# Spreading a norm's factor over the partitions by a store and a broadcast load instead of matmuls with the identity, in six norms of a two-layer streaming encoder

## Chip, cores and metric

The kernel runs on one core of a Trainium2 chip. The metric is the device time of one execution in microseconds (us); lower is better. The engines are TensorE (PE), VectorE (DVE), ScalarE (ACT), GpSimd (POOL) and SyncE (SP), which here issues the DMAs. The line numbers in the text are those of the kernel before, L163 for line 163, unless it says otherwise.

## What is computed

Two layers of an encoder over 1056 tokens (1024 of a prompt and 32 of a sample) of width 1024, in float32. Around each layer's mixer stand two norms: one of the layer's input, and one of its output before the residual is added. These norms are what the change touches.

```python
def rmsnorm(x, g):
    xf = x.astype(jnp.float32)
    y = xf * lax.rsqrt(jnp.mean(xf * xf, axis=-1, keepdims=True) + RMS_EPS)
    return (y * g.astype(jnp.float32)).astype(x.dtype)
...
    for layer in range(DEPTH):
        if layer % 2 == 0:
...
            yp, pp, kp, vp = even_mixer(rmsnorm(xp, norm_pre[layer]), *wts)
...
        else:
...
            yp, cp, np_, mp = odd_mixer(rmsnorm(xp, norm_pre[layer]), *wts)
...
        xp = xp + rmsnorm(yp, norm_post[layer])
```

The even layer's mixer is a combined input projection, a pooling branch and a chunk-band attention, then an output projection; the odd layer's is an input projection, an mLSTM and an output projection.

## The kernel before

Activations lie transposed: the 1024 channels as eight blocks of 128 partitions, the tokens along the free dimension. The tokens are worked on in three groups, GR: two of 384 tokens (group 0 and 1) and one of 288 (group 2). A float32 matrix product is made of three matmuls, L108 to L110: activations and weights are split into a high and a low part (xh, xl and wh, wl), and xh by wh, xl by wh and xh by wl are summed in PSUM.

A norm needs, for each token, r = 1 / sqrt(mean of squares + eps), and needs it on every partition, since tokens lie along the free dimension and r multiplies the 128 channels of a block.

- The squares of the eight blocks are added up as they come: ACT squares (L193, tiles sqt and th), POOL adds to the tile acc (L194). This is `sumsq`.
- `rnorm_p` then sums over the partitions on PE: with acc as the stationary operand and one column of ones, each 128 tokens give one column of 128 sums (L163). The tokens now lie on the partitions. DVE makes mean + eps (L170, L172, tile rn_a), and `rsqrt` takes POOL's power of -0.5 (L182, rn_b) and one Newton step on DVE (L183 to L185). At the end of L185 the tile y, or rn_b, holds r, token 128 c + p on partition p in column c.
- To bring r back on the free dimension and onto all partitions, PE multiplies once for each 128 tokens: column c of y, broadcast to 128 columns, is the stationary operand and the identity the moving one (L176). Every partition of the PSUM tile pm then holds r of the tokens. `rnorm` copies it to SBUF on ACT (L153), into the tile rp or r.

Two kinds of norm call this outside the first layer's input. `out_proj` makes one for each group behind the output projection: at k = 0 of the group's second pass it calls `rnorm` into rp (L804), and each of the eight blocks y is then multiplied by rp (L808), the residual x0, loaded at L807, is added (L809), and `finish` is called. This second pass runs while PE already works on the next group. In layer 0, `finish` is `fin0` (L1166): it stores the new x to DRAM (L1172, x1d), splits it for the next layer's projection (L206 xh, L209 xl), adds up its squares, and after the eighth block calls `rnorm` for the next layer's input norm, into the tile r1 (L1176, r in the trace). r1 is not applied to x but to the projection's result in PSUM, when DVE evacuates it (L263, L265). In layer 1, `finish` is `fin1`: it stores the result (L1180, out_y). Group 2 of layer 1 takes another way, `out_last` (L813), with x0 loaded at L820.

At the boundary of the layers, three more things matter. `gate_rows` (L837) multiplies the new x of each group with the weights of the gates, sixteen matmuls a group (L846, L847), and the PSUM tile is evacuated by a copy on ACT (L849) and an addition on DVE (L850). The weights come in blocks of 128 x 512 by a load on SP (L94, wr), a conversion on ACT (L95, wh) and a subtraction on DVE or POOL (L96, wl); the gates' own weights are split at L835 and L836. And each engine works its instructions off in the order in which the scheduler put them; it places an instruction by what it expects to be ready, so an edit to one norm can shift the order of its neighbours. SP's queue is in order too: a store that waits for its data holds back every load behind it.

Of the kernel before, what the change touches and what calls it, by code (L numbers as in the profile page):

```python
# [7 lines left out]
F32 = mybir.dt.float32  # L8
# [25 lines left out]
class Net:  # L34
    def __init__(self, tc, io):
        self.tc = tc
        self.nc = tc.nc
        self.io = io
        self.due = []
        self.store = None  # L40


# [106 lines left out]
        return xh, xl  # L149


    def rnorm(self, acc, n, out, col=None, pool=None):
        self.nc.scalar.copy(out=out, in_=self.rnorm_p([acc], n, col, pool))  # L153

    def rnorm_p(self, accs, n, col=None, pool=None):
        nc = self.nc
        p = self.pn.tile([128, 512], F32, name="pm") if pool is None else pool.tile([128, 512], F32, name="pv")
        nf, rem = n // 128, n % 128
        nq = nf + (rem > 0)
        for c in range(nq):  # L160
            L = min(128, n - 128 * c)
            for i, acc in enumerate(accs):
                nc.tensor.matmul(out=p[:L, 400 + c:401 + c], lhsT=acc[:, 128 * c:128 * c + L], rhs=self.ones[:, 0:1],  # L163
                                 start=i == 0, stop=i == len(accs) - 1)
        ms = self.tp.tile([128, 4], F32, name="rn_a", bufs=2)
        y = self.tp.tile([128, 4], F32, name="rn_b", bufs=2) if col is None else col
        u = self.tp.tile([128, 4], F32, name="rn_c", bufs=2)
        if rem:
            nc.vector.memset(ms, 1.0)
            nc.vector.tensor_scalar(out=ms[:rem, nf:nq], in0=p[:rem, 400 + nf:400 + nq], scalar1=1.0 / 1024, scalar2=1e-6,  # L170
                                    op0=ALU.mult, op1=ALU.add)
        nc.vector.tensor_scalar(out=ms[:, :nf], in0=p[:, 400:400 + nf], scalar1=1.0 / 1024, scalar2=1e-6, op0=ALU.mult, op1=ALU.add)  # L172
        self.rsqrt(y[:, :nq], ms[:, :nq], u[:, :nq])
        for c in range(nq):
            L = min(128, n - 128 * c)
            nc.tensor.matmul(out=p[:, 128 * c:128 * c + L], lhsT=y[:L, c:c + 1].to_broadcast([L, 128]), rhs=self.ident[:L, :L],  # L176
                             start=True, stop=True)
        return p[:, :n]
# [554 lines left out]
    def out_proj(self, wsrc, gpost, late, resid, finish, ytiles=(), nx0=4, nopen=2, end=False, w2=2, anchor=None):  # L733
        nc = self.nc
        tc = self.tc
        mv = self.mix.rearrange("(k p) t -> p k t", p=128)
        early = [k for k in range(8) if k not in late]
        steps = []
        ws = []
        ytiles = list(ytiles)  # L740
        for gi in range(3):
            s, n = GR[gi]
            x = self.new_x(gi)
            for k in early + list(late):
                if k in late:
                    src = late[k][:, s:s + n]
                else:
                    xr = self.tp.tile([128, 384], F32, name="xr", bufs=4)
                    with tc.issue_after(wdma) if gi and 1 else nullcontext():
                        nc.sync.dma_start(out=xr[:, :n], in_=mv[:, k, s:s + n])  # L750
                    src = xr[:, :n]
                with tc.issue_after(anchor) if gi and anchor is not None else nullcontext():
                    self.split_x(x, k, src, None, nc.gpsimd if gi < 2 and k % 2 == 0 else None)
            acc = self.tp.tile([128, 384], F32, name="acc", bufs=2)
            ys = []
            accs = [acc[:, :n]]

            def evac(m, p):
                if gi == 0 and ytiles:
                    y = ytiles.pop(0)  # L760
                else:
                    y = self.lp.tile([128, 384], F32, name="y", bufs=11)
                ys.append(y)
                if end and gi == 2 and m == 7:
                    sq = self.tp.tile([128, 384], F32, name="sqt", bufs=2)
                    nc.scalar.activation(out=sq[:, :n], in_=p, func=AF.Square)
                    accs.append(sq[:, :n])
                else:
                    self.sumsq(acc[:, :n], p, n, m == 0)
                nc.scalar.mul(out=y[:, :n], in_=p, mul=gpost[:, m:m + 1])  # L770
            batches = [list(range(nopen))] + [[m] for m in range(nopen, 8)] if gi == 0 else [[m] for m in range(8)]
            for ms in batches:
                opened = []
                for m in ms:
                    while gi == 0 and len(ws) <= min(ms[-1] + 1, 7):
                        i = len(ws)
                        ws.append(self.load_w(wsrc[i], None if i < 2 else w2 if i == 2 else i))
                        if i == 6:
                            wdma = self.wdma
                        if i == 4 and self.store is not None:  # L780

                            with tc.issue_after(self.wdma):
                                self.store()
                            self.store = None
                    w = ws[m]
                    p = (self.pn.tile([128, 512], F32, name="pm") if gi == 0 and m == 3 and end else self.pd.tile([128, 512], F32, name="pd"))[:, :n]
                    self.mm3(p, w, x, early, True, False)
                    opened.append((m, w, p))
                for m, w, p in opened:
                    self.mm3(p, w, x, list(late), False, True)  # L790
                    evac(m, p)
                for _ in range(2):
                    if steps:
                        steps.pop(0)()
            while steps:
                steps.pop(0)()
            if end and gi == 2:
                self.out_last(ys, accs, resid, s, n, finish)
                return
            r = self.lp.tile([128, 384], F32, name="rp", bufs=1)  # L800

            def one(k, gi=gi, s=s, n=n, ys=ys, acc=acc, r=r):
                if k == 0:
                    self.rnorm(acc[:, :n], n, r[:, :n])  # L804
                y = ys[k][:, :n]
                x0 = self.lp.tile([128, 384], F32, name="x0", bufs=nx0)
                nc.sync.dma_start(out=x0[:, :n], in_=resid[128 * k:128 * k + 128, s:s + n])  # L807
                nc.vector.tensor_tensor(out=y, in0=y, in1=r[:, :n], op=ALU.mult)  # L808
                nc.vector.tensor_tensor(out=y, in0=y, in1=x0[:, :n], op=ALU.add)  # L809
                finish(gi, k, y)  # L810
            steps = [lambda k=k, one=one: one(k) for k in range(8)]
        return steps

# [340 lines left out]
    def run(self):  # L1154
        tc, nc, io = self.tc, self.nc, self.io
        with tc.tile_pool(name="cp", bufs=1) as self.cp, tc.tile_pool(name="xp", bufs=1) as self.xp, \
# [8 lines left out]
            accs = {}  # L1165

            def fin0(gi, k, y):
                s, n = GR[gi]
                if k == 0:
                    x1[gi] = self.new_x(gi)  # L1170
                    accs[gi] = self.tp.tile([128, 384], F32, name="acc", bufs=2)
                nc.sync.dma_start(out=x1d[128 * k:128 * k + 128, s:s + n], in_=y)  # L1172
                self.split_x(x1[gi], k, y, self.g_pre[1])
                self.sumsq(accs[gi][:, :n], y, n, k == 0, None, "th")
                if k == 7:
                    self.rnorm(accs[gi][:, :n], n, r1[:, s:s + n])  # L1176

            def fin1(gi, k, y):
                s, n = GR[gi]
# [2 lines left out]
            with tc.tile_pool(name="la", bufs=1, reuse_waits="tile") as self.la:  # L1182
                with tc.tile_pool(name="lq", bufs=1, reuse_waits="tile") as self.lq:
# [4 lines left out]
                    with tc.tile_pool(name="lp0b", bufs=1, reuse_waits="tile") as self.lp, tc.tile_pool(name="pn", bufs=2, reuse_waits="tile", space=PSUM) as self.pn:  # L1188
                        next(l0)
                        r1 = self.tp.tile([128, T], F32, name="r", bufs=1)  # L1190
# [100 lines left out]
```

## Time and profile before

| what | value |
| --- | --- |
| median of three runs | 1215.55 us (1214.6 to 1216.65) |
| the profiled execution, its own time | 1215.28 us |
| its span, first to last instruction | 1213.6 us |
| mean granted clock of PE, as a share of full speed | 0.991 |
| PE busy | 1183.3 us, 98% |
| DVE, ACT, POOL busy | 681.2, 472.9, 298.9 us |

Busy times of engines overlap. An engine that is idle costs nothing unless the chain that ended last runs through it. PE's matmuls are pipelined: one of 384 columns is listed with 0.33 us, but the next begins 0.17 us after it.

### The profile page before, as it was taken

To read this page: it belongs to the slowest core of one execution; us is meant where nothing else is said; L and a number is where in the kernel's file an instruction comes from. 1 tells how busy PE (TensorE), PEld (TensorE's weight loads), DVE (VectorE), ACT (ScalarE), POOL (GpSimd) and SP (SyncE) were. 2 spreads that over 40 slices of the span, in tenths; PEclk is the share of its full clock that TensorE was granted. 3 is DMA by queue.
4 is the path that set the end of the run, shared out by engine and by line. 5 is a ranking of instruction groups with operands and counts; after the bars stand their busy time and mean duration, and the time that the engine had idled before them with its cause. 6 is when DMAs were issued, how large, how long until landed. Compare 5 with 4: busy or idle time off the path is not lost.

```text
span 1213.6 us, 19521 instructions
## 1 busy us (share of the span) xinstructions
PE 1183.3 (98%) x7457; PEld 1137.1 (94%) x7457; DVE 681.2 (56%) x1460; ACT 472.9 (39%) x980; POOL 298.9 (25%) x394
## 2 busy tenths in 40 slices
PE   7899999999999899999999999999999999999996
PEld 7899899898899799999999899999999999998996
DVE  7657476576668446774447533753247432666424
ACT  7624334443533454531334232432234322445521
POOL 1323532433241335620102300221003110123322
PEclk9999999999999999999999899999999999999998
DMA  8401121112212253321111231122111321122433
GB/s 257 125 19 54 54 82 53 54 45 67 78 36 92 80 176 105 124 94 53 54 36 53 63 101 36 52 67 98 36 51 42 76 88 36 44 77 79 128 104 130
DMA packets 79613, 94.03 MB, mean 77 GB/s; under 512 B 19208, under 2 KB 56856, under 8 KB 79520
## 3 DMA queue, kind: packets, MB, share of 16 engines
q1 hardware_dynamic: 79520, 92.79, 24.9%
q8 instruction: 58, 0.95, 0.3%
q14 instruction: 35, 0.29, 0.1%
HBM read 72.64 MB, written 21.69 MB: 78 GB/s over the span
## 4 chain that ended last, share of the span: by engine, by line
PE 95%; ACT 1%; DMA 1%; DVE 1%; issue 1%; POOL 1%; SPq 0%; DVEq 0%; POOLq 0%; ACTq 0%
PE pd L108 25%; PE pd L110 25%; PE pd L109 25%; PE pv L406 4%; PE ps L354 1%; PE pm L950 1%; PE ps L355 1%; PE ps L1018 1%; PE pv L985 1%; PE pv L987 1%; PE pv L986 1%; PE ps L985 1%; PE ps L986 1%; PE ps L987 1%; PE pm L176 1%
## 5 line engine op out<-in xcount | busy, mean ns | idle before, releaser
L108 PE MATMUL pd<-xh,wh 128*128 128x384 f32 (+1 forms) x1864 | 610.2, 328 | 9.4 <-ACT wh L95 7.8
L110 PE MATMUL pd<-xh,wl 128*128 128x384 f32 (+1 forms) x1864 | 607.5, 326 | 0.1
L109 PE MATMUL pd<-xl,wh 128*128 128x384 f32 (+1 forms) x1864 | 607.1, 326 | 0.1
L108 PEld LDWEIGHTS pd<-xh,wh 128*128 128x128 f32 x1864 | 352.4, 189 | 13.6 <-ACT wh L95 8.1
L109 PEld LDWEIGHTS pd<-xl,wh 128*128 128x128 f32 x1864 | 352.6, 189 | 2.6 <-POOL xl L203 0.3
L110 PEld LDWEIGHTS pd<-xh,wl 128*128 128x128 f32 x1864 | 352.3, 189 | 2.4 <-DVE wl L96 0.7
L95 ACT CAST wh<-wr 128x512 fp32r<-128x512 f32 x158 | 91.4, 619 | 154.6 <-PE pd L109 109.6
L96 DVE TENSOR_TENSOR wl<-wr,wh 128x512 fp32r<-128x512 f32 x116 | 78.2, 701 | 22.1 <-ACT wh L95 20.5
L96 POOL TENSOR_TENSOR wl<-wr,wh 128x512 fp32r<-128x512 f32 x42 | 55.7, 1342 | 83.4 <-DMA extr<-ext 27.4
L194 POOL TENSOR_TENSOR acc<-acc,sqt 128x384 f32<-128x384 f32 (+1 forms) x41 | 43.5, 1062 | 88.2 <-ACT sqt L193 88.1
L1032 POOL TENSOR_TENSOR qal<-qa,qah 128x256 fp32r<-128x256 f32 (+1 forms) x32 | 27.5, 863 | 141.1 <-ACT qah L1031 130.3
L75 POOL TENSOR_SCALAR_AFFINE_SELECT D<-D 128x128 f32<-128x128 f32 (+1 forms) x36 | 12.2, 340 | 181.2 <-ACT D L1014 168.1
L406 PE MATMUL pv<-st,vt 128*128 128x512 f32 (+1 forms) x192 | 55.1, 433 | 0.9 <-ACT rg L415 0.9
L406 PEld LDWEIGHTS pv<-st,vt 128*128 128x128 f32 x192 | 35.0, 189 | 20.3 <-issue 10.6
L263 DVE TENSOR_TENSOR row<-pd,r 128x384 f32<-128x384 f32 (+1 forms) x36 | 18.3, 520 | 59.4 <-PE pd L110 59.3
L372 ACT ACTIVATE st<-ps,far 128x256 f32<-128x256 f32 (+3 forms) x56 | 27.1, 489 | 50.0 <-DVE st L364 34.0
L1050 DVE SCALAR_TENSOR_TENSOR C<-C,MA,ps 128x258 f32<-128x258 f32 x64 | 30.4, 478 | 28.8 <-PE ps L987 17.8
L265 DVE SCALAR_TENSOR_TENSOR kT<-pd,r 128x384 f32<-128x384 f32 (+1 forms) x24 | 12.6, 524 | 57.4 <-PE pd L110 57.3
L395 DVE TENSOR_TENSOR st<-st,mb 128x512 f32<-128x512 f32 (+1 forms) x96 | 39.3, 485 | 8.3 <-POOL mb L699 8.3
L1030 POOL TENSOR_TENSOR qa<-qT,MA 128x128 f32<-128x128 f32 (+1 forms) x64 | 26.9, 439 | 66.1 <-DVE qT L263 35.9
L364 DVE TENSOR_TENSOR st<-ps,B 128x256 f32<-128x256 f32 (+1 forms) x72 | 25.3, 371 | 24.7 <-PE ps L355 24.3
L1085 ACT ACTIVATE hn<-num,n_u,n_y 128x256 f32<-128x256 f32 (+1 forms) x36 | 20.4, 596 | 40.9 <-PE pv L1087 34.3
(305 smaller groups left out, 1681.5 us busy)
## 6 DMA issues: line engine op xcount, KB each, us to landing
wr<-in_w SPq DMA_DIRECT2D x128, 256.0 KB, 3.0
xr<-mix SPq DMA_DIRECT2D x26, 192.0 KB, 2.5
wr<-in_w0o SPq DMA_DIRECT2D x16, 256.0 KB, 3.2
MA<-mdr SPq DMA_DIRECT2D x32, 128.0 KB, 3.5
wr<-in_w1o SPq DMA_DIRECT2D x16, 256.0 KB, 3.3
x<-in_x SPq DMA_DIRECT2D x16, 192.0 KB, 2.8
x<-x1d SPq DMA_DIRECT2D x16, 192.0 KB, 3.5
out_y<-y SPq DMA_DIRECT2D x16, 192.0 KB, 2.0
```

The costliest lines, as they stand in the source:

```text
L95: nc.scalar.copy(out=wh[:, k], in_=wr)
L96: eng.tensor_tensor(out=wl[:, k], in0=wr, in1=wh[:, k].bitcast(F32), op=ALU.subtract)
L108: nc.tensor.matmul(out=p, lhsT=wh[:, k], rhs=xh[:, k], start=first and i == 0, stop=False)
L109: nc.tensor.matmul(out=p, lhsT=wh[:, k], rhs=xl[:, k], start=False, stop=False)
L110: nc.tensor.matmul(out=p, lhsT=wl[:, k], rhs=xh[:, k], start=False, stop=last and i == len(ks) - 1)
L194: (eng or nc.gpsimd).tensor_tensor(out=acc, in0=acc, in1=t[:, :n], op=ALU.add)
L372: nc.scalar.activation(out=st[:, off + a:off + b], in_=p[:, a:b], func=AF.Identity, bias=far)
L395: nc.vector.tensor_tensor(out=dst, in0=dst, in1=mb[:, a - q0:b - q0], op=ALU.subtract)
L406: nc.tensor.matmul(out=pv[:, a - q0:b - q0], lhsT=vt[:, j, 64 * e:64 * e + 128], rhs=dst, start=(i == 0), stop=(i == len(order) - 1))
L1030: nc.gpsimd.tensor_tensor(out=qa[:, d, :L], in0=qT[:, d, t], in1=Ab, op=ALU.mult)
L1032: nc.gpsimd.tensor_tensor(out=qp[1], in0=qa[:, :, :L], in1=qp[0].bitcast(F32), op=ALU.subtract)
L1050: nc.vector.scalar_tensor_tensor(out=Cn[:, d], in0=C[:, d], scalar=Ab[:, L - 1:L], in1=pu, op0=ALU.mult, op1=ALU.add)
```

## The change

In two places, for groups 0 and 1 alone, `rnorm` is replaced by `rnorm_far`. It runs `rnorm_p` up to the end of the Newton step (a new argument, `spread=False`, returns there), into a tile of its own, rn_d. Then it stores the 128 x 3 numbers to a row of 384 numbers in DRAM, in the order of the tokens, so that each number goes to a place of its own, and loads this row into rp or r1 on all 128 partitions, a broadcast of 192 KB. Both DMAs are issued by SP. The matmuls of L176 and the copy of L153 are gone for these norms: six of them, groups 0 and 1 of the output norm of layer 0, of the input norm of layer 1 and of the output norm of layer 1. Group 2 and the first layer's input norms stay as they are.

```diff
@@ -37,6 +37,7 @@
         self.due = []
+        self.nfar = 0
         self.store = None
@@ -149,10 +150,23 @@
+    def rnorm_far(self, acc, n, out):
+        nc = self.nc
+        y = self.tp.tile([128, 4], F32, name="rn_d", bufs=2)
+        self.rnorm_p([acc], n, y, spread=False)
+        nf, rem = n // 128, n % 128
+        row = self.dr.tile([1, 384], F32, name=f"rfar{self.nfar}")
+        self.nfar += 1
+        nc.sync.dma_start(out=row[0, 0:128 * nf].rearrange("(c p) -> p c", p=128), in_=y[:, :nf])
+        if rem:
+            nc.sync.dma_start(out=row[0, 128 * nf:n].rearrange("(p c) -> p c", c=1), in_=y[:rem, nf:nf + 1])
+        nc.sync.dma_start(out=out, in_=row[0:1, 0:n].to_broadcast([128, n]))
+
     def rnorm(self, acc, n, out, col=None, pool=None):
         self.nc.scalar.copy(out=out, in_=self.rnorm_p([acc], n, col, pool))
 
-    def rnorm_p(self, accs, n, col=None, pool=None):
+    def rnorm_p(self, accs, n, col=None, pool=None, spread=True):
@@ -171,6 +185,8 @@
         self.rsqrt(y[:, :nq], ms[:, :nq], u[:, :nq])
+        if not spread:
+            return
         for c in range(nq):
@@ -801,7 +817,7 @@
                 if k == 0:
-                    self.rnorm(acc[:, :n], n, r[:, :n])
+                    (self.rnorm_far if gi < 2 else self.rnorm)(acc[:, :n], n, r[:, :n])
@@ -1173,7 +1189,7 @@
                 if k == 7:
-                    self.rnorm(accs[gi][:, :n], n, r1[:, s:s + n])
+                    (self.rnorm_far if gi < 2 else self.rnorm)(accs[gi][:, :n], n, r1[:, s:s + n])
```

The changed kernel's lines are 1 to 16 further down (its L161 is the store, its L164 the load). What moves on the engines' queues beyond that is shown at three places.

SP's queue between the two norms that stand 7 us apart, the layer-1 input norm of group 0 and the layer-0 output norm of group 1. Before:

```order
L1172 DMA x1d<-y 128x384
L807 DMA x_4829<-in_x 128x384
L94 DMA wr<-in_w 128x512 x3
L1172 DMA x1d<-y 128x384 x4
L807 DMA x_4869<-in_x 128x384
```

After:

```order
L823 DMA x_4826<-in_x 128x384
L161 DMA rfar_4565<-rn_d 128x3x1
L164 DMA r<-rfar_4565 128x384
L95 DMA wr<-in_w 128x512 x2
L161 DMA rfar_4762<-rn_d 128x3x1
L95 DMA wr<-in_w 128x512
L164 DMA rp<-rfar_4762 128x384
L1188 DMA x1d<-y 128x384 x4
```

Both pairs stand ahead of the next stores of x; a weight load stands between the second store and its load.

PE's queue at the sums over the partitions of the layer-1 input norm of group 0 (pm<-ones,acc). Before:

```order
L108 MATMUL pd<-xh_4306,wh_4236 128x384
L109 MATMUL pd<-xl_4307,wh_4236 128x384
L110 MATMUL pd<-xh_4306,wl_4237 128x384
L108 MATMUL pd<-xh_4306,wh_4236 128x384
L109 MATMUL pd<-xl_4307,wh_4236 128x384
L163 MATMUL pm<-ones,acc 128x1 x3
L110 MATMUL pd<-xh_4306,wl_4237 128x384
```

After:

```order
L110 MATMUL pd<-xl_4307,wh_4197 128x384
L111 MATMUL pd<-xh_4306,wl_4198 128x384
L109 MATMUL pd<-xh_4306,wh_4236 128x384
L110 MATMUL pd<-xl_4307,wh_4236 128x384
L111 MATMUL pd<-xh_4306,wl_4237 128x384
L109 MATMUL pd<-xh_4306,wh_4236 128x384
L110 MATMUL pd<-xl_4307,wh_4236 128x384
L177 MATMUL pm<-ones,acc 128x1 x3
L111 MATMUL pd<-xh_4306,wl_4237 128x384
```

The sums now stand behind five matmuls of the weight block 4236 instead of fourteen, so nine matmuls earlier. On POOL, the additions of squares are reordered alike: one addition of sqt (L194) that stood ahead of the norm's last addition now stands behind it. The sums of the next norm, of group 1, stand six matmuls of 288 columns further back than before, and those of the layer-1 input norm of group 1 four matmuls of 384 columns further back.

PE's queue at the gate rows of groups 0 and 1 (x of group 0 is xl_4388 and xh_4387 before). Before:

```order
L163 MATMUL pm<-ones,acc 32x1
L108 MATMUL pd<-xh_5119,wh 128x288
L109 MATMUL pd<-xl_5120,wh 128x288
L110 MATMUL pd<-xh_5119,wl 128x288
L847 MATMUL pd<-xh_4387,wh 128x384
L846 MATMUL pd<-xl_4388,wh 128x384
L847 MATMUL pd<-xh_4387,wh 128x384
L846 MATMUL pd<-xl_4388,wh 128x384
L847 MATMUL pd<-xh_4387,wh 128x384
L846 MATMUL pd<-xl_4773,wh 128x384
```

After, where group 1's x is xl_4770 and xh_4769:

```order
L110 MATMUL pd<-xl_5116,wh 128x288
L111 MATMUL pd<-xh_5115,wl 128x288
L862 MATMUL pd<-xl_4770,wh 128x384
L863 MATMUL pd<-xh_4769,wh 128x384
L862 MATMUL pd<-xl_4770,wh 128x384
L863 MATMUL pd<-xh_4769,wh 128x384
```

Before, the last five matmuls of group 0's gate rows stood directly ahead of group 1's. Now all sixteen of group 0 stand in one piece further ahead, and group 1's follow a stretch of group 2's projection. On ACT, the evacuation of group 1's gate rows (L849) now stands behind a fourth conversion of weights (L95), where it stood ahead of it.

## Rows read from the trace of the kernel before

**Rows 1.** The page: busy time of PE; the chain that ended last, by engine.

```profile
PE 1183.3 (98%) x7457; PEld 1137.1 (94%) x7457; DVE 681.2 (56%) x1460; ACT 472.9 (39%) x980; POOL 298.9 (25%) x394
...
PE 95%; ACT 1%; DMA 1%; DVE 1%; issue 1%; POOL 1%; SPq 0%; DVEq 0%; POOLq 0%; ACTq 0%
```

**Rows 2.** Instructions of L176: count of records, duration ns min/median/max, first and last start.

```profile
L176 PE MATMUL pm<-ident,rn_b x54: 271/275/376, 456.5 to 1205.0; 128*128 128x128 f32 x48, 32*128 32x32 f32 x6
```

**Rows 3.** The chain in order of time, 440 to 560 us: start us, us, what.

```profile
456.68 0.67 PE pm L176 x6
...
478.75 0.83 PE pm L163 x6
...
513.04 1.51 PE pm L163 x12
```

**Rows 4.** Timeline of DVE: start us, us, line, operation, [idle before <-releaser].

```profile
457.90 2.43 DVE L808 TENSOR_TENSOR qT<-qT,rp 128x384 f32<-128x384 f32 x5 [4.76 <-ACT rp L153]
...
488.36 0.16 DVE L185 SCALAR_TENSOR_TENSOR rn_b<-rn_c,rn_b 128x3 f32<-128x3 f32 x1
...
492.34 3.99 DVE L808 TENSOR_TENSOR y<-y,rp 128x384 f32<-128x384 f32 x7 [1.95 <-ACT rp L153]
...
513.07 0.56 DVE L263 TENSOR_TENSOR qT<-pd,r 128x384 f32<-128x384 f32 x1 [1.73 <-PE pd L110]
...
515.43 0.16 DVE L185 SCALAR_TENSOR_TENSOR rn_b<-rn_c,rn_b 128x3 f32<-128x3 f32 x1
...
520.66 0.56 DVE L263 TENSOR_TENSOR qT<-pd,r 128x384 f32<-128x384 f32 x1 [4.23 <-ACT r L153]
...
1184.76 2.58 DVE L808 TENSOR_TENSOR y<-y,rp 128x384 f32<-128x384 f32 x4 [4.09 <-ACT rp L153]
```

**Rows 5.** Timeline of SP's issues and of ACT at a store and its broadcast load.

```profile
587.69 0.32 SPq L931 DMA_DIRECT2D mdr<-num  x1
...
589.94 1.41 SPq L1010 DMA_DIRECT2D MA<-mdr  x3
...
593.25 0.40 ACT L1014 ACTIVATE D<-MA,g_c 128x128 f32<-128x128 f32 x1 [5.56 <-DMA MA<-mdr]
```

**Rows 6.** DMA issues of the whole span: count, KB each, median us to landing.

```profile
xr<-mix SPq DMA_DIRECT2D x26, 192.0 KB, 2.5
...
extr<-ext SPq DMA_DIRECT2D x8, 192.0 KB, 4.1
...
out_uo<-u SPq DMA_DIRECT2D x8, 7.5 KB, 2.6
...
mix<-smo SPq DMA_DIRECT2D x4, 16.0 KB, 1.4
```

**Rows 7.** Timelines of POOL and PE around the sums of the layer-1 input norms.

```profile
476.07 1.34 POOL L194 TENSOR_TENSOR acc<-acc,sqt 128x384 f32<-128x384 f32 x1
477.37 1.33 POOL L194 TENSOR_TENSOR acc<-acc,th 128x384 f32<-128x384 f32 x1
...
511.98 1.01 POOL L194 TENSOR_TENSOR acc<-acc,th 128x384 f32<-128x384 f32 x1
...
478.33 0.34 PE L109 MATMUL pd<-xl,wh 128*128 128x384 f32 x1
```

**Rows 8.** Timeline of DVE: the split of the gates' weights.

```profile
489.70 0.69 DVE L836 TENSOR_TENSOR wh<-wr,wh 128x512 fp32r<-128x512 f32 x1 [1.18 <-ACT wh L835]
```

**Rows 9.** Timelines of PE, ACT and DVE at the gate rows.

```profile
539.93 0.44 PE L846 MATMUL pd<-xl,wh 128*128 128x384 f32 x1 [1.15 <-DVE row L850]
...
540.49 0.62 ACT L95 CAST wh<-wr 128x512 fp32r<-128x512 f32 x1 [1.19 <-DMA wr<-in_w]
...
543.55 0.55 DVE L850 TENSOR_TENSOR row<-pd,row 64x384 f32<-64x384 f32 x1 [1.71 <-ACT row L849]
```

**Rows 10.** Timeline of ACT in group 2 of the last projection.

```profile
1192.30 1.04 ACT L770 ACTIVATE y<-pd,vec 128x288 f32<-128x288 f32 x2 [0.57 <-DMA out_y<-y]
1194.48 0.41 ACT L193 ACTIVATE sqt<-pd 128x288 f32<-128x288 f32 x1 [1.15 <-PE pd L110]
```

## The prediction

> **What bounds the kernel now.** I read the page's busy table and chain first [rows 1]: TensorE (PE) is busy 98% of the span and makes 95% of the chain that ends last. An instruction taken off PE's queue therefore shortens the kernel by its own time, unless a wait takes its place. Next, what the change removes. The matmuls with the identity, line 176, that use this kind of norm have 54 records, six for each of nine norms [rows 2]; on the chain, one norm's six cost 0.67 us (456.68) [rows 3]. Six norms change; I call them A, C, B, D (at 453, 481, 488 and 515 us: group 0 of layer 0's post-norm, group 0 of layer 1's pre-norm, then the same two for group 1) and E, F (layer 1's post-norm, 1146 and 1180 us). If nothing else moved, the gain would be 6 x 0.67 = 4.0 us.
>
> Then I looked at who waits for r. VectorE (DVE) does nothing between the norm's last step, L185, and the first use of r [rows 4]: from 453.14 to 457.90 us for A (4.76), 488.52 to 492.34 for B (3.82), 515.59 to 520.66 for D (5.1) and 1180.66 to 1184.76 for F (4.1). C's r is first used at 513.07, some 30 us after its norm. E is of A's kind. In these waits the norm stands behind other matmuls in PE's queue; PE's own share is 0.67, and ACT copies the result. So the question is what a store and a load take, against 3.8 to 5.1 us.
>
> **The price of the round trip.** No row of this trace shows a 1.5 KB store spread over 128 partitions in 4-byte pieces, so X, the time from L185's end to a usable r, is bounded. The nearest row is the same idiom: a 16.5 KB store at 587.69, the broadcast load that reads it issued at 589.94 (2.25 later), and ScalarE (ACT) released by it at 593.25 (3.31 after that) [rows 5]: 5.56 us. That load was one of several in flight; here it is alone. A load of the same 192 KB without broadcast takes 2.5 us (xr) [rows 6], which makes 2.25 + 2.5 = 4.75. I take **X = 5.2**, the middle of these two. The far bounds: the fastest small store, 1.4, and xr make 3.9; the store that is made of the smallest pieces, out_uo with 2.6, and the 192 KB broadcast extr with 4.1 make 6.7 [rows 6].
>
> **The change, step by step.** I keep a ledger: PE's time after the change minus before, at the same work.
>
> A: its matmuls go, -0.67. Its r comes 5.2 - 4.76 = 0.44 later, and the chain y*r, plus residual, square, add follows.
>
> C: its sums, line 163, wait for GpSimd's (POOL) last add, which ended at 477.37 + 1.33 = 478.70, with PE there at about 478.5, its last matmul having begun at 478.33 [rows 7]. In the new order these sums stand nine matmuls of 0.172 us earlier (1.55) and one square's add (1.34) fewer stands ahead of the last one. PE arrives at 478.5 - 0.67 - 1.55 = 476.3; the add ends at 478.70 - 1.34 + 0.44 = 477.8. PE waits 1.5 us, and with the nine matmuls still to do it stands at 477.8 + 1.55 - 478.75 = **+0.6**. A's gain is gone here. C's own matmuls then go: -0.1.
>
> B: its sums now stand behind six more matmuls of 288 columns, at three quarters of 0.172 each, 0.8 in all. y is ready at 488.52 + 0.7, r at 494.4, which is 2.1 later than before. On SyncE's (SP) queue a weight load that waits for L836's split at 489.70 [rows 8] now stands between store and load; it ends at 490.4, before the store has landed (489.2 + 2.25), so I cost it at nothing. If the store landed sooner than that, it would hold the load. Weight loads may share the transfer's time with it; the upper bound of X holds that. B's matmuls go: -0.75.
>
> D: its sums had no slack at all: POOL's last add ended at 511.98 + 1.01 = 512.99 and PE went on at 513.04 [rows 3, 7]. Of B's 2.1 us about 0.4 is taken up by POOL's queue, where the last adds of the squares stand back to back; the sums start at 514.7, and four matmuls (0.69) that came behind them are now ahead: 514.7 - 513.04 - 0.69 = **+1.0**. D's own matmuls go: +0.3. D's r comes at 515.59 + 1.66 + 5.2 = 522.45, 1.8 later, and DVE, which idles for it (4.23), starts group 2's residual work that much later.
>
> The gate rows: PE stood idle 1.15 us at 539.93 for an evacuation of the gate rows [rows 9]. The new order puts all sixteen matmuls of group 0's gate rows ahead of other work, and that stall should go: -0.85. But the next pair is held by ACT: line 849 of group 1 now stands behind a fourth weight conversion, which at 540.49 waits for its load. And what follows group 2's gate rows, the first k matmuls, now waits for those rows' evacuation, a copy and an add of about 0.45 each for 288 columns. Before, they waited for no evacuation, and the one at 543.55 (0.55 for 384 columns) stood ahead of the sixteen [rows 9]. So a wait of about 0.9 behind takes the place of one in front; it comes out even if the sixteen start at 543.2 instead of 544.1, and by the shifts above I have them start between 543.2 and 543.7. I put A to D together at **+0.1** (-0.2 to +0.5).
>
> E: r 0.4 later, but what waits for it is a multiplication and the stores of y, beside group 1's projection, whose matmuls fill the 30 us up to F: **-0.67**. F: r comes 5.2 - 4.1 = 1.1 later. The stores of y follow it, and ACT's evacuation in group 2 already waits for one of them at 1192.30 (0.57) [rows 10]; the first of those two evacuations ends at 1192.82, and PE takes that buffer again at 1194.48, where the tile before ended: 1.66 to spare, 1.0 when PE is 0.67 ahead. So 0.1 is lost: **-0.6**. The ACT copies (one for each norm), and twelve DMA issues on SP, which issues nothing in most of the time here, cost nothing as long as nothing behind a waiting store is due; behind F's stand loads of group 2's residual, not needed for 15 us.
>
> Sum: 0.1 - 0.67 - 0.6 = -1.2 us. The profiled run took 1215.28 us (span 1213.6), 0.3 under the median of the runs: **1214.1**. A measurement of this kernel tells 0.2%, 2.4 us, from no change: the forecast is no change.
>
> **Rivals.** Each us of X is worth about 3 us above 5.2: A's delay reaches C's sums and through PE also B's norm, B's reaches D's sums, and F's reaches PE; below 5.2 it is about 2, since F's and part of B's are then hidden.
>
> (1) The round trip is short and hidden. At X = 4.0, about the low bound, A and F wait no longer than before, and the time is 1214.1 - 2 x 1.2 = 1211.7. Everything hidden and the stalls at C and 539.93 gone too would be 4.0 + 0.25 + 1.15 = 5.4, or 1209.9. For it: DVE waited 3.8 to 5.1 us already. Against: the one round trip in the trace took 5.56. The Trainium skill, "DMA: Bandwidth & Descriptors", section "Anatomy of one DMA — SWDGE (gpsimd) path", gives a fixed cost of about 2.0 us for each transfer, and by it two small ones would take about 4.0; the rows here lie above that, 2.25 and 2.5 to 4.1. Chance 0.28.
>
> (2) Slower: the store in 4-byte pieces is dear. The store's 384 pieces are three times out_uo's (128 partitions with 60 bytes each; its 7.5 KB takes 2.6 us where 192 KB of xr take 2.5 [rows 6], so pieces and not bytes set it). With 3.2 for the store and the broadcast's 3.5 to 4.1, X is 6.7 to 7.3. At 6.7, 1.5 x 3 = 4.5 comes on top: 1218.6. It is slower from X = 6.4 on (-1.2 + 3 x 1.2 = 2.4). Its place is B's r and D's sums at 513. The Trainium skill, same page, section "Rules for kernel authors", speaks against this change: a transfer whose last dimension is strided becomes one descriptor per element. No row here shows the price of that. Chance 0.22.
>
> (3) The order of PE, not X, decides: the sums moved nine matmuls earlier cost the 1.5 us stall, and the 1.15 at 539.93 doesn't go, or comes back behind the gate rows. Then A to D come to +1.2 and the time is 1215.2: no change either. Chance 0.12.
>
> That the matmuls stay can be excluded: PE's order has 18 of them fewer, in six places.
>
> **How the numbers follow.** My forecast has 0.38. No change within 0.2%: 0.38 + 0.12 less the tails, 0.48; faster 0.30, since the forecast's lower tail adds 0.02; slower 0.22. The range takes X from 4.0 with some of the stalls gone (1211.7 - 1.0) to 6.5 (1214.1 + 3.9): 1210.7 to 1218.0.
>
> **What would show it.** Line 176's 54 records should fall to 18. DVE's idle before L808 (A, B) and L263 (D) should read 5.2, and B's use of r start at about 494. PE should wait about 1.5 us before C's sums, near 476 to 478, and as long before D's. The stall at the gate rows of 539.93 should be gone and a smaller one stand ahead of the first k matmuls. Outside 440 to 560 us and the last 70 us both traces should agree. X under 4.5 or over 6.4 makes the forecast wrong, and so does a stall of PE of over 2 us anywhere behind D.

## The result, and the profile after

The changed kernel takes 1260.62 us (median of 4 runs, 1259.16 to 1261.74) beside 1216.05 us before: a ratio of 1.0364 (95% interval 1.0348 to 1.0379), 45 us slower, where no change was forecast. Its profiled execution has a span of 1258.6 us and a mean granted clock of 0.974.

The page of the changed kernel, busy times and chain; beside [rows 1] PE's share of the chain falls from 95% to 78%, and DMA has 11%:

```profile
PE 1192.7 (95%) x7421; PEld 1143.2 (91%) x7421; DVE 675.0 (54%) x1460; ACT 469.0 (37%) x974; POOL 296.8 (24%) x394
...
PE 78%; DMA 11%; DVE 5%; ACT 3%; issue 2%; POOL 1%; SPq 1%; DVEq 0%; ACTq 0%; POOLq 0%
```

The matmuls went as said: 36 records fewer. What took their place is in the view of DMA issues (count, KB each, median us from issue to landing):

```profile
rp<-rfar SPq DMA_DIRECT2D x4, 192.0 KB, 4.9
...
rfar<-rn_d SPq DMA_DIRECT2D x6, 1.5 KB, 8.4
```

The store of 1.5 KB lands after 8.4 us, the load takes 4.9: X, the time from the norm's end to a usable r, is 13.3, where 5.2 was taken and 6.7 was the far bound. DVE's idle time before the first use of r is about that long, 12.5 to 15.9 us, on the lines that answer to [rows 4] (norms A, B, D and F; idle in brackets). B's is the longest; its store took 11.8 us.

```profile
467.57 2.43 DVE L824 TENSOR_TENSOR qT<-qT,rp 128x384 f32<-128x384 f32 x5 [13.58 <-DMA rp<-rfar]
...
516.10 3.84 DVE L824 TENSOR_TENSOR y<-y,rp 128x384 f32<-128x384 f32 x8 [15.92 <-DMA rp<-rfar]
...
553.17 0.56 DVE L279 TENSOR_TENSOR qT<-pd,r 128x384 f32<-128x384 f32 x1 [12.49 <-DMA r<-rfar]
...
1229.60 2.90 DVE L824 TENSOR_TENSOR y<-y,rp 128x384 f32<-128x384 f32 x6 [13.74 <-DMA rp<-rfar]
```

PE stands idle six times where it did not before (timeline of PE, idle in brackets):

```profile
476.18 0.44 PE L109 MATMUL pd<-xh,wh 128*128 128x384 f32 x1 [3.89 <-ACT y L786]
486.03 0.83 PE L177 MATMUL pm<-ones,acc 128*128 128x1 f32 x6 [2.96 <-POOL acc L210]
...
524.54 0.61 PE L109 MATMUL pd<-xh,wh 128*128 128x288 f32 x1 [12.81 <-ACT y L786]
...
557.67 1.24 PE L109 MATMUL pd<-xh,wh 128*128 128x288 f32 x2 [5.95 <-ACT xh L222]
...
1200.47 0.44 PE L109 MATMUL pd<-xh,wh 128*128 128x384 f32 x1 [1.73 <-ACT y L786]
...
1236.45 0.61 PE L109 MATMUL pd<-xh,wh 128*128 128x288 f32 x1 [7.44 <-ACT y L786]
```

Four of the six wait for ACT's evacuation L786, that is for a free PSUM buffer. The two of them at the boundary of the layers, 476.18 and 524.54, have one cause: ACT takes its instructions in order, and there the next one was the split of the late x (timeline of ACT for the longer stall; the evacuation is the second line). The two in layer 1, 1200.47 and 1236.45, have another, the buffers y, which the experiments show. Of the other two, the stall at 486.03 stands at C's sums, and the one at 557.67 waits for group 2's x, which DVE makes behind its wait for D's late r.

```profile
520.44 0.61 ACT L222 ACTIVATE xh<-y,vec 128x384 fp32r<-128x384 f32 x1 [14.60 <-DVE y L825]
...
524.00 0.87 ACT L786 ACTIVATE y<-pd,vec 128x288 f32<-128x288 f32 x2
```

And behind each stall PE runs slower. The view of windows (PE busy and records, granted clock, DMA share, GB/s) shows clocks between 0.60 and 0.84 around the stalls, where 1.0 is the upper of the two levels, 2.4 GHz, and 0.5 the lower, 1.2 GHz; the matmul of 288 columns at 524.54 is listed with 0.61 us, where those of the kernel before take 0.30 in the mean:

```profile
470.00:480.00 10.00, 6.11 (x28) 0.84 0.55 178
480.00:490.00 10.00, 7.04 (x34) 0.84 0.44 138
510.00:520.00 10.00, 1.72 (x13) 0.72 0.24 21
520.00:530.00 10.00, 5.46 (x29) 0.60 0.61 207
```

**Where the 45 us are.** PE's idle time (span less busy) rises from 30.3 to 65.9 us, by 35.6. Its busy time rises by 9.4, though 4.0 us of matmuls are gone, so the matmuls that are left take 13.4 longer: 35.6 + 13.4 - 4.0 = 45.0. The six stalls above make 34.8 of the 35.6. By place: the sums over the partitions are landmarks on the chain in order of time. In the kernel before, those of B and E:

```profile
485.69 0.56 PE pm L163 x6
...
1144.38 0.56 PE pm L163 x6
```

and after, B, D (the one that answers to 513.04 in [rows 3]) and E:

```profile
496.26 0.56 PE pm L177 x6
...
537.58 0.58 PE pm L177 x6
...
1177.89 0.58 PE pm L177 x6
```

The lag is 10.6 us at B's sums (A's late r), 24.5 at D's (B's added), 33.5 at E's (D's added) and 45.0 at the end (E's and F's). Some 0.75 of it stood at A's sums already, before any r was late (451.39 against 450.64).

### The profile page after: what moved, and what is told of

Its sections match the earlier page's. It is cut to its first block, busy times and chain, and to the rows that moved or that the text cites. A ratio compares the mean times of both kernels' runs of the same rounds, so it can differ in the third digit from the quotient of the medians.

```text
span 1258.6 us, 19464 instructions
## 1 busy us (share of the span) xinstructions
PE 1192.7 (95%) x7421; PEld 1143.2 (91%) x7421; DVE 675.0 (54%) x1460; ACT 469.0 (37%) x974; POOL 296.8 (24%) x394
## 4 chain that ended last, share of the span: by engine, by line
PE 78%; DMA 11%; DVE 5%; ACT 3%; issue 2%; POOL 1%; SPq 1%; DVEq 0%; ACTq 0%; POOLq 0%
PE pd L109 21%; PE pd L110 20%; PE pd L111 20%; PE pv L422 4%; DMA rfar<-rn_d 4%; DMA rp<-rfar 2%; DMA MA<-mdr 1%; DMA wr<-in_w 1%; PE ps L370 1%; PE pm L966 1%; PE ps L371 1%; PE ps L1034 1%; PE pv L1001 1%; PE pv L1003 1%; PE pv L1002 1%
## 5 line engine op out<-in xcount | busy, mean ns | idle before, releaser
L76 POOL TENSOR_SCALAR_AFFINE_SELECT D<-D 128x128 f32<-128x128 f32 (+1 forms) x36 | 12.5, 348 | 180.8 <-ACT D L1030 168.4
L1066 DVE SCALAR_TENSOR_TENSOR C<-C,MA,ps 128x258 f32<-128x258 f32 x64 | 30.3, 477 | 29.7 <-PE ps L1003 17.3
L380 DVE TENSOR_TENSOR st<-ps,B 128x256 f32<-128x256 f32 (+1 forms) x72 | 25.4, 371 | 25.8 <-PE ps L371 25.3
L824 DVE TENSOR_TENSOR y<-y,rp 128x384 f32<-128x384 f32 (+1 forms) x33 | 15.1, 527 | 43.0 <-DMA rp<-rfar 43.0
```

The source lines that it names most:

```text
L1066: nc.vector.scalar_tensor_tensor(out=Cn[:, d], in0=C[:, d], scalar=Ab[:, L - 1:L], in1=pu, op0=ALU.mult, op1=ALU.add)
```

## The experiments

Twelve kernels were run; each group had runs of the kernel before beside it. Four causes were to be told apart: the store's small pieces, any round trip through DRAM, SP's queue, and the new order on PE.

**What makes the store late.** One unused store behind each norm, in six shapes (A to F and the others in turn):

```diff
+        if i % 6 == 0:
+            out, src = row[0:384].rearrange("(c p) -> p c", p=128), y[:, 0:3]
+        elif i % 6 == 1:
+            out, src = row[0:384].rearrange("(p c) -> p c", c=3), y[:, 0:3]
+        elif i % 6 == 2:
+            out, src = row[0:128].rearrange("(p c) -> p c", c=1), y[:, 0:1]
+        elif i % 6 == 3:
+            out, src = row.rearrange("(c p s) -> p c s", p=128, s=16)[:, :, 0], y[:, 0:3]
...
+        self.nc.sync.dma_start(out=out, in_=src)
```

> The kernel before, with one extra store behind each of its nine norms that nobody reads or waits for, in six shapes: 384 pieces of 4 bytes side by side (as in the change), 128 pieces of 12 bytes side by side, 128 pieces of 4 bytes, 384 pieces of 4 bytes each 64 bytes from the next, 3 pieces of 512 bytes, 128 pieces of 12 bytes each 64 bytes apart. Theory (the small pieces make the store slow to land): the first shape lands in 8.4 us here too, the 128 pieces in 2.5 to 4, the 3 pieces in about 2; if the 384 spread pieces also take 8, their number decides, if they take 2 to 3, that neighbours share a place in DRAM. The time stays within 2.4 us of before, since nobody waits. Rival (any small store of r lands this late, because of what else runs on the DMA engines then): all shapes 7 to 9 us.

The trace shows a landing for four of the stores (DMA issues in short windows, in order of time):

```profile
prb<-rn_b SPq DMA_DIRECT2D x1, 1.5 KB, 3.0
...
prb<-rn_b SPq DMA_DIRECT2D x1, 0.5 KB, 6.9
...
prb<-rn_b SPq DMA_DIRECT2D x1, 1.5 KB, 3.2
...
prb<-rn_b SPq DMA_DIRECT2D x1, 1.5 KB, 2.1
```

The first and the last are 128 pieces of 12 bytes side by side (3.0 and 2.1), the second 128 pieces of 4 bytes side by side (6.9, where 2.5 to 4 was expected), the third 384 pieces of 4 bytes, each 64 bytes from the next (3.2). The change's own shape and the last two of the list show no landing in this run. With a load behind it that nobody uses (the unused pair, below), the change's own shape lands after 7.8 to 8.2 us in five of six places. So it is not the number of pieces that makes the store late, since 384 spread ones land in 3.2 (one store, with no other DMA beside it), but that 4-byte pieces are neighbours. The 6.9 fits this but decides nothing: the DMA engines were 81% busy with weight loads then. The time was 1218.9 us, ratio 1.003 (1.0019 to 1.0041), a little more than expected; where these 2.5 us went was not followed.

**The same change with a faster store.** The sums take every third token, so that a partition holds three neighbours:

```diff
-        self.rnorm_p([acc], n, y, spread=False)
+        self.rnorm_p([acc[:, :n].rearrange("q (p c) -> q c p", c=3)], n, y, spread=False)
...
-        nc.sync.dma_start(out=row[0, 0:128 * nf].rearrange("(c p) -> p c", p=128), in_=y[:, :nf])
+        nc.sync.dma_start(out=row[0, 0:128 * nf].rearrange("(p c) -> p c", c=3), in_=y[:, :nf])
```

> The changed kernel with the sums over the partitions taken of every third token, so that a partition holds three neighbouring tokens and the store is 128 pieces of 12 bytes instead of 384 of 4. Nothing else is different. Theory (pieces): the store lands in 3 to 4 us instead of 8.4, r comes 8 to 9 us after its norm instead of 13.3, and of the 45 us lost some 10 to 15 are left: 1225 to 1232. Rival (a store and a dependent load through DRAM cost this much in any shape, or the new order of PE is what costs): 1255 to 1262.

1225.51 us, ratio 1.0074 (1.0048 to 1.0100). DMA issues:

```profile
rp<-rfar SPq DMA_DIRECT2D x4, 192.0 KB, 4.0
...
rfar<-rn_d SPq DMA_DIRECT2D x6, 1.5 KB, 2.2
```

With 6 us taken off the store, 35 of the 45 us are gone, with the sums of the changed norms on PE within one matmul of the change's order: the pieces make most of the loss, not the order and not the round trip as such. But 9 us are left at X = 6.2 to 6.5. The windows say in what:

```profile
470.00:480.00 10.00, 7.46 (x44) 1.00 0.59 190
480.00:490.00 10.00, 10.00 (x57) 0.83 0.16 22
```

PE idles 6.3 us more than before (36.6 against 30.3), and its matmuls take 8.9 us longer, behind stalls of no more than 2.6 us. Not all of this is the clock: the sums of every third token take PE 0.32 us more a norm (shown below for E's), some 1.9 us for six. How much of the 9 us is the new order on PE was not separated from the rest.

**SP's queue alone.** The kernel before with the store and load at the six places, into a tile that nobody reads:

```diff
+        if col is None and n == 384:
+            self.pair(y)
...
+    def pair(self, y):
+        row = self.dr.tile([1, 384], F32, name=f"rfar{self.nfar}")
...
+        nc.sync.dma_start(out=row[0, 0:384].rearrange("(c p) -> p c", p=128), in_=y[:, :3])
+        nc.sync.dma_start(out=d, in_=row[0:1, 0:384].to_broadcast([128, 384]))
```

> The kernel before, r still made by the matmuls with the identity, and at the six changed norms the same store and broadcast load on SP's queue besides, into a tile that nobody reads. Theory (r's lateness costs, and SP's queue only little): within 5 us of before, 1214 to 1220, since what stands behind the pair on SP's queue is late by up to 9 us but mostly has that much to spare. Rival (SP's queue: stores of x, residual loads and weight loads held behind the waiting load are what stops PE): 1235 or more, over half of the 45 us.

1227.81 us, ratio 1.0096 (1.0074 to 1.0119): over twice what the theory allowed, and still a quarter of the 45 us. It lies between what the theory and the rival said. One stall makes most of it. Timelines of SP, ACT and PE:

```profile
491.19 0.39 SPq L188 DMA_DIRECT2D rfar<-rn_b  x1
502.67 0.33 SPq L189 DMA_DIRECT2D rdead<-rfar  x1
503.09 0.38 SPq L95 DMA_DIRECT2D wr<-in_w  x1
503.56 1.90 SPq L1183 DMA_DIRECT2D x1d<-y  x4
...
509.06 0.50 ACT L781 ACTIVATE y<-pd,vec 128x288 f32<-128x288 f32 x1 [7.90 <-DMA x1d<-y]
...
509.61 0.61 PE L109 MATMUL pd<-xh,wh 128*128 128x288 f32 x1 [6.79 <-ACT y L781]
```

r was in time here. But the load waits for the store on SP, the stores of x stand behind the load, and ACT's evacuation needs a buffer y that such a store must first empty. This is a second way in which the slow store can reach PE, and it was costed at nothing. In the changed kernel it is hidden: ACT there waits for the late x itself (520.44 above), so these 11.4 us are not to be added to what the late r costs. B's store took 11.5 us between its issue and the load's (11.8 in the changed kernel), where A's took 7.8; two weight loads had been issued directly before it.

**Layer 1's two norms alone, and what stops PE there.**

```diff
-                    (self.rnorm_far if gi < 2 else self.rnorm)(acc[:, :n], n, r[:, :n])
+                    (self.rnorm_far if gi < 2 and end else self.rnorm)(acc[:, :n], n, r[:, :n])
```

with the layer-1 input norms back at `rnorm`.

> The change in the two output norms of layer 1 alone; the four norms at the boundary of the layers keep the matmuls. Theory (each late r stops PE by itself, as the trace after shows: up to the sums of the first of these two norms the changed kernel is 33.5 us behind, at its end 45): 45 - 33.5 = 11.5 us over before, 1225 to 1229. Rival (the new order of PE and ACT at the boundary costs the rest of the kernel, too): 1214 to 1218.

1227.6 us, ratio 1.0095 (1.0074 to 1.0116), 11.2 over before, as expected. To this kernel, matmuls without use were added where PE idled:

```diff
+                    if end and gi == 2 and m == 6:
+                        idle = self.pn.tile([128, 512], F32, name="pm")
+                        self.mm3(idle[:, :n], w, x, range(8), True, True)
+                        self.mm3(idle[:, :n], w, x, range(5), True, True)
                     self.mm3(p, w, x, early, True, False)
```

> The kernel with the change in layer 1's two output norms alone, and 39 extra matmuls of 288 columns ahead of the seventh product of group 2, where PE then stood idle for 6.4 us; their result is not used. Theory (a stall of PE costs twice, by itself and by the lower clock behind it): the extra matmuls take 5.4 us of the stall at 0.137 us each and lengthen nothing; the granted clock from 1200 to 1210 us, 0.62 to 0.70 without them, stays near 1.0, and the two products behind the stall take 6.6 us instead of 8.7, so 1224.5 to 1226 against 1227.6 without them. Rival (the stall alone costs; the clock falls with what DMA and the other engines do there): the clock falls as before and the time is 1227.6 or more.

1225.27 us, ratio 1.0073 (1.0056 to 1.0091); the spans are 1225.5 without and 1222.4 with the 39 extra matmuls, but 0.9 of these 3.1 us stood ahead of this stage already. The stall falls from 6.40 to 1.55 us, and from its end to the sums of the last norm it is 7.2 us instead of 9.2 (1202.97 to 1210.19, and 1203.56 to 1212.75). Windows without them:

```profile
1200.00:1205.00 5.00, 1.44 (x6) 0.62 0.64 228
1205.00:1210.00 5.00, 5.00 (x29) 0.70 0.93 286
```

and with them:

```profile
1200.00:1205.00 5.00, 3.45 (x26) 1.00 0.76 272
1205.00:1210.00 5.00, 4.74 (x37) 1.00 0.90 266
```

More work, and no more time: the clock follows what PE did before, not the DMA traffic, which is alike. The two intervals overlap, so the time alone would not show a gain; the clock of the windows does. Next, the same kernel with more buffers instead:

```diff
-                    y = self.lp.tile([128, 384], F32, name="y", bufs=11)
+                    y = self.lp.tile([128, 384], F32, name="y", bufs=(11 if not end else 16))
```

> The kernel with the change in layer 1's two output norms alone (1227.6 us), with 16 buffers instead of 11 for the projection's results y, so that an evacuation in group 2 needs no buffer whose store waits for r. Theory (the late r stops PE through the buffers: r, then y, then the store of y, then ACT's evacuation into that buffer, then PE's next product): both stalls of PE in this stage, 1.0 and 6.4 us, go and with them the low clock behind the second; what is left is the residual of group 2, whose loads stand on SP's queue behind the stores that waited for r. They land by about 1212.4, some 4 us later than PE needs them. 1217 to 1221. Rival (PE is stopped by the late r in another way): 1226 or more.

1216.57 us, ratio 1.0005 (0.9996 to 1.0014): the 11 us are gone, more than expected, though r is as late as ever (DVE waits 25.8 us for it in two places, 25.3 with 11 buffers). What is gone is the wait of ACT's evacuation for the store of a y, in the kernel with 11 buffers:

```profile
1203.00 1.03 ACT L786 ACTIVATE y<-pd,vec 128x288 f32<-128x288 f32 x2 [8.54 <-DMA out_y<-y]
```

So in layer 1 the late r reached PE through the buffers y, and what other way there may be costs under 2 us. With 12-byte pieces besides:

> The change in layer 1's two output norms alone, with the store in pieces of 12 bytes and 16 buffers for y. Theory (a late r costs nothing where the buffers cover it, and the matmuls with the identity were on PE's path): both norms' 0.67 us are gained, 1213.5 to 1215.5 beside a before of 1215.7. Rival (what is saved on PE there only makes the last norm wait longer): the same as with 4 bytes, 1216 to 1217.

1216.55 us, ratio 1.0004 (0.9994 to 1.0013): as the rival said, and not the gain of the theory. But there was less to gain than the 1.33 us of matmuls, since this layout has a price on PE. The sums of every third token take 0.90 us to the next matmul, where those of neighbouring tokens take 0.58 (timeline of PE at E's sums, here and in the run before this one):

```profile
1146.25 1.04 PE L177 MATMUL pm<-ones,acc 128*128 128x1 f32 x6
1147.15 0.42 PE L111 MATMUL pd<-xh,wl 128*128 128x384 f32 x1
...
1145.53 0.72 PE L177 MATMUL pm<-ones,acc 128*128 128x1 f32 x6
1146.11 0.42 PE L111 MATMUL pd<-xh,wl 128*128 128x384 f32 x1
```

That leaves 0.7 us in two norms, 0.06%, and the interval doesn't rule it out. Whether it was gained is not shown.

**One norm at a time at the boundary.** First the one whose r has time, with 12-byte and with 4-byte pieces (`gi < 1` in place of `gi < 2` for the layer-1 input norm, the others at `rnorm`):

> The change in one norm alone, that of layer 1's input for group 0, whose r is first used some 30 us after it, with the store in pieces of 12 bytes. The other five keep the matmuls. Theory (what costs is a late r, and here it is not late): 0.67 us of matmuls saved and nothing lost, -0.7 us, 1214.5 to 1217 beside a before of 1216.4. Rival (the round trip costs by SP's queue wherever it stands): 1218.5 or more.

> The same one norm, with the change's own store of 384 pieces of 4 bytes. Its load holds SP's queue some 8 us, in which three weight loads fall due (486.57 us in the trace before). Theory (a pair on SP's queue costs only where something behind it is due at once; the pair of the next norm 7 us later was the one that stopped PE): the weight loads go 3 to 4 us later, PE waits 0 to 2 us for them, 1215 to 1219. Rival (the head of SP's queue is the main cost): 1221 or more, a quarter of the 45 us or so.

1218.27 us, ratio 1.0014 (1.0003 to 1.0025), and 1218.26 us, 1.0010 (1.0001 to 1.0020): 1 to 2 us over before, and no gain; the first was expected at 1217 or less, the second lies in its range. The store's shape makes no difference where r has time: with 4 bytes the weight loads are issued at 490.09 instead of 486.35 and nothing waits for them. The loss isn't at the norm either. The 4-byte kernel comes to the gate rows level with before (539.92 and 539.93), and 86 us on, at the same stall of PE, it is 1.5 us behind (625.42 and 623.91). At the gate rows PE's stall is 1.45 us in both kernels, 1.15 before [rows 9], and the clock falls behind it (the rows are the 12-byte kernel's; the other has 0.83 too, and the kernel before 1.00 with 62 matmuls):

```profile
540.34 0.44 PE L862 MATMUL pd<-xl,wh 128*128 128x384 f32 x1 [1.45 <-DVE row L866]
540.00:550.00 10.00, 9.66 (x51) 0.83 0.29 94
```

Why this stall is 0.3 us longer was not followed. Then the first norm, A, alone (`gi < 1 and not end`):

> The change as it is, 4 bytes, in one norm alone, layer 0's output norm for group 0, the first of the six. Theory (each late r stops PE by itself): as in the trace after, where PE stood 3.9 us for a free buffer and 3.0 us for the sums of the next norm, and ran at half its rate in between, 10.6 us behind at the sums after that: 1222 to 1227, a fifth of the 45 us. Rival (the four late norms at the boundary only cost because each one's pair holds the next one's on SP's queue): within 3 us of before.

1226.64 us, ratio 1.0081 (1.0065 to 1.0096): 10.6 us, as much as the changed kernel's lag at B's sums. Waits of PE from 440 to 580 us (total, times, longest):

```profile
PE pm L177 <- POOL acc L210: 3.0, 1, 3.0
PE pd L109 <- ACT y L786: 2.8, 1, 2.8
```

5.8 us of waits cost 10.6; the clock from 470 to 490 is 0.83.

**r without a second way through PE.** Two attempts at a better kernel: ones in 128 columns as the stationary operand give the sums on all partitions at once (in the second, ACT takes the root and DVE the reciprocal).

```diff
+        nc.tensor.matmul(out=p[:, :n], lhsT=self.ones, rhs=acc, start=True, stop=True)
...
+        nc.gpsimd.tensor_tensor(out=out, in0=ms[:, :n], in1=self.mhalf[:, 0:1].to_broadcast([128, n]), op=ALU.pow)
```

> The kernel before; in the six norms the sums over the partitions are taken with 128 columns of ones as the stationary operand and the squares as the moving one, so that every partition holds the sums of all tokens and neither matmuls with the identity nor a round trip is needed. The root and the Newton step then run on 128 x 384 numbers instead of 128 x 3. PE saves the sums' 0.56 us in each of six norms (3.4 us in all). Theory (r's time decides): latency is 0.67 on PE, three DVE steps of about 0.55 and one before, and POOL's power on 384 columns, of which no trace shows the price (0.86 for 3 columns). If that takes 3 us or less, r is as early as with the matmuls and the time is 1211 to 1215; if it takes 8 us or more, r is as late as with the round trip and the time 1225 or more. Rival (only the lost matmuls count): 1211 to 1213 whatever POOL takes.

1577.19 us, ratio 1.2962. POOL's power on 384 columns is the reason (lines view: busy, mean ns, idle before):

```profile
L187 POOL TENSOR_TENSOR rp<-sqt,mhalf 128x384 f32<-128x384 f32 x4 | 246.2, 61546 | 8.9 <-DVE sqt L186 8.9
```

```diff
+        nc.scalar.activation(out=ms[:, :n], in_=p[:, :n], func=AF.Sqrt, scale=1.0 / 1024, bias=self.eps)
+        nc.vector.reciprocal(out=out, in_=ms[:, :n])
```

> As the run with the sums on all partitions, but the root is taken by ACT, straight from PSUM, and DVE makes the reciprocal; no Newton step, and POOL has no part in it. ACT loads a function table three times for it. r is then 0.67 (PE) + 0.5 (ACT) + the reciprocal, of which no trace shows the price, behind the sums; one way through PE's queue instead of two. Theory (r's time decides, and PE's matmuls count where nothing waits): if the reciprocal takes 0.6 to 1 us, r comes 3 us earlier than before, PE saves 0.56 us in each of six norms and most of the stall at the gate rows' place: 1210 to 1214. If it takes 3 us or more: 1214 to 1218. Rival (table loads on ACT, 1.3 us each, hold evacuations and cost more than that): 1217 or more.

1223.58 us, ratio 1.0061 (1.0048 to 1.0073), above both ranges of the theory. The number fits the rival, its cause does not: after the first of the three table loads (450.86) PE is only 0.3 us behind at B's sums, and 7.3 at 631.25. The reciprocal takes 2.55 us, and in the new order D's sums stand 48 matmuls earlier on PE, ahead of their data:

```profile
508.85 1.65 PE L185 MATMUL pm<-acc,ones 128*128 128x384 f32 x2 [4.39 <-POOL acc L204]
```

No version here beats the kernel before.

## Why the prediction was wrong

**The step that failed is the price of the round trip**, and of its two terms the store. X was taken as 5.2 with 6.7 as the far bound; it is 13.3. The store's term was 2.25 and came out as 8.4. The load's, about 3 with 4.1 as its bound [rows 6], came out as 4.9, and as 4.0 with the short store. The 2.25 were read from a store of four rows of 1056 numbers (L931) [rows 5], so of long pieces. The store's bound, 2.6, was read from pieces of 60 bytes, and rival 2 took 3.2 for three times as many. That is also what 384 pieces take when they lie 64 bytes apart, which is luck; side by side they take 8.4. The rival had the right mechanism and sign ("the store in 4-byte pieces is dear"), but a bound that is worked out from another shape was used as if it held for this one. The sentence from the Trainium skill, "DMA: Bandwidth & Descriptors", section "Rules for kernel authors", that a strided last dimension becomes one descriptor per element, agrees: the trace has 400 packets in the 2 us from a store's issue, about one for each of the 384 numbers.

**The worth of a us of X was too low, 3 where about 5 was measured** (1260.6 less 1225.5 over 7 us of X, in two kernels that differ in the store and in the tokens that a sum takes). A right X alone would not have saved the forecast: at X = 6.3 its working gives 1214.1 + 1.1 x 3 = 1217.4, and the kernel with the short store takes 1225.5. Three things are missing from the working. The granted clock has no term in it: 13.4 of the 45 us are slower matmuls, and the clock falls behind the stalls, as the filled stall shows. The path at the boundary is another than the one through the sums: A's and B's late r stopped PE for 3.9 and 12.8 us because ACT had the split of the late x ahead of an evacuation. Only 3.0 us of the stalls stand at sums, at C's, and none at D's, where rival 2 had its place. And at B the pair on SP's queue was costed at nothing, since the weight load behind it was not late; the stores of x behind the load were (the unused pair, 11.4 us by itself).

**E** was given -0.67 as having time. It stopped PE for 1.73 us, through the buffers y, and so did F with 7.4; the prediction had this path, but only for F.

**What held.** C's sums stall was forecast as 1.5 us from the order; it is 2.96 with X = 13.3, and 2.5 with 12-byte pieces, so it is there but larger. Of the 54 records of line 176 of before, 18 are left. The stall for a gate-row evacuation did leave the place it had, but not as said: it stands ahead of group 2's gate rows, 1.5 us at 574.90, and not ahead of the first k matmuls. Outside the two stretches named, the lag grows little: of the 33.5 us at E's sums 33.0 stand at 656.90 already, and layer 1's norms alone make 11.2. And where the round trip had time, C alone or E and F with more buffers, it cost no more than 1 to 2 us and gained nothing that shows.

## What to carry to other kernels

Before r, or any small vector, goes through DRAM, look at how the pieces lie there: put neighbours into one partition, so that the pieces grow and get fewer, and count what that layout costs elsewhere (here 0.32 us of PE a norm). Look, too, at what is due on the queue behind the waiting load; another queue for it was not tried here. A late operand costs by the path on which it reaches the busy engine: here ACT's order and the buffers y, and five more buffers took away 11 us where the latency stayed. When a stall of a few us on PE is weighed, the slower matmuls behind it belong in the sum; they were 13.4 us beside 35.6 of stall.

## What the runs showed of the hardware

- A store of 384 neighbouring 4-byte pieces lands 7.7 to 8.9 us after its issue, and 11.5 to 11.8 directly behind two weight loads, though its 400 packets (norm A) had all gone through the DMA engines within 1.4 us of it; 128 pieces of 12 bytes side by side land in 2.0 to 3.1 us, one store of 4-byte pieces 64 bytes apart in 3.2. That neighbours collide in one place of DRAM fits these numbers, but no run shows the collision itself.
- POOL's power takes 61.5 us for 128 x 384 numbers and 0.94 for 128 x 3 (mean of nine); DVE's reciprocal of 128 x 384 takes 2.55 us, against 0.55 for a multiplication.
- A short stall of PE can bring its lower clock behind it, and doesn't always: around the 1.5 us at 574.90 the window from 570 to 580 us shows 0.83, behind the 1.45 us with C alone that from 540 to 550 us shows 0.83, and behind the 1.15 us in the kernel before [rows 9] that from 540 to 560 us shows 1.00.
- Sums over the partitions with every third token as the stationary operand's columns take PE 0.90 us for 384 tokens, with neighbouring tokens 0.58.
